# A decoder block with product-key experts: 32 instead of 64 tokens by fetched rows, and another order of four steps

## The chip, the cores and the metric

The kernel runs on one core of one Trainium2 chip. Times are device microseconds (us) of one execution. TensorE multiplies (PE in the profile, PEld its weight loads), VectorE is DVE, ScalarE is ACT, GpSimd is POOL and issues the indirect DMAs, SyncE is SP and issues the other DMAs.

## The reference

512 tokens of width 1024, float32 throughout:

```
h   = adaLN(RMSNorm(x), c);  p = h @ W_in            # q | k | v | conv B, C, u
attn = sliding window (128), 8 query heads on 2 key heads, RMSNorm on q and k, rotary, sinks
conv = B * conv3_causal(C * u)
x  += gate1 * ([RMSNorm(attn) | RMSNorm(conv)] @ W_out)
h2  = adaLN(RMSNorm(x), c)
x  += gate2 * PEER(h2)
```

PEER has 16384 experts of one neuron each, an expert being a row of `u` and a row of `v`. A token has 8 heads; a head picks 16 of 128 keys on each of two sides, and then the 16 best of the 256 sums. So each token has 128 experts: `out = sum_k g_k * gelu(u_k . h2) * v_k`.

## The kernel before, in words

The float32 products are made of float32r parts: a helper (`split`, lines 175 to 177) has ACT write the high part `hi` and DVE the low part `lo` of every weight tile, and `mm3` (lines 197 to 202) issues three matmuls (L200, L201, L202) for each of 8 tiles of 128.

The tokens are dealt with in two ways. The first 384 (`TD`, three chunks of 128) are "dense": for them whole tables are multiplied. Expert number is 128*j + i in the order of the kernel, and `first()` (line 606) takes one of 128 columns j: it loads 512 KB of `u`, splits it, and makes 24 matmuls into `pa`, whose width is the number of dense tokens that are served so, `TU` = 384 - `HT` = 320. ACT puts a gelu on it. The first `SPILL` = 66 columns go out to memory in pairs (`Ad`) and come back later (`sp`), the others stay in a ring of 4 pairs (`ge`). `second()` (line 966) takes one column of `v`: it is loaded and split, and multiplied by the gated activations `w` of all three chunks in 18 matmuls of 512 (L977 to L979) into six PSUM banks that stay open over all 128 columns. The gates stand in `Gd`, which 24 steps of `build()` (line 902, 16 tokens each) make from the routing with one-hot products on DVE (L912 to L927) and 32 small matmuls each into `gps`.

The last 64 dense tokens (`HT`) do not get their `u` products from `first()`. `last_dense()` (line 780) fetches, for each of 64 steps, 128 rows of `u` by an indirect DMA on POOL (tile `row` from `in_uR` by `eH`, 512 KB) and makes one dot product in each partition on DVE (L778, by `hN`): a step serves 64 tokens with two experts each. `eH` and `wN` are moved between the two halves of the partitions by one small DMA each. What is left is a gating factor that goes into the routing slots (L794 to L802).

The last 128 tokens are "gathered" (`gathered()`, line 854): their routing (`route`, two halves of four heads), then 128 fetches of `u` rows with a dot each (L778, by `h2N`), and 128 fetches of `v` rows with a multiply-add each (L893). This runs beside the rest in portions: `todo` counts units, a step of the main loop adds some and the generator gives back what its pieces are put down at (1.4 for one top-16 search of five DVE operations, 1.9 for the second search, 2.5 for a lookup, 1.3 for a dot or multiply-add).

The order of the main part: 2 columns of `first()`; six lookups of the dense routing (line 810) with `LOOK` = 4 columns each and, from the second lookup on, two dots of `last_dense()` each; the turned routing of the three chunks (lines 822 to 835, PSUM tile `ijg`, then `jI`, `jl` and the slots); 24 builds (lines 1004 to 1016), the first 16 with two columns and three dots, the last 8 with one column, two dots at most and, from build 20, 1.7 units of `gathered()`; 6 more columns with 2.3 units each; then 66 columns of `second()` without a `first()` (1.85 units each, `PACE`), 56 with one (4.4 units each), and 6 more. The attention (lines 374 to 432) comes long before that: `attend1` makes the scores of 8 heads (`sc`, L383, 64 partitions deep, head group g in the upper or lower half of the partitions), `attend2` turns them (L415), copies them (L417) and multiplies by `vN` (`po`, L423, 64 columns of weights per group).

The order in each engine's queue is not quite that of the program text: a planner in the framework writes the queues when the program is built, by its own estimates of durations, taking the earliest step of the text that is ready. The chip is given the queues as written. `after(ins, mark)` adds a wait for another instruction, and `fetch` (line 767) makes row fetches wait for the last matmul of a `second()`.

Of the kernel before, what the change touches and what calls it, by code (L numbers as in the profile page):

```python
# [11 lines left out]
I32 = mybir.dt.int32  # L12
# [12 lines left out]
TD = ND * P  # L25
HT = 64
TU = TD - HT
# [7 lines left out]
GS = 32768.0  # L35
RING = 4
LOOK = 4
SPILL = 66
EARLY = 1
# [5 lines left out]
WHEN = (-1, 0, 2, 3)  # L45
PACE = (1.85, 4.4)

# [42 lines left out]
def body(tc, p):  # L90
# [283 lines left out]
    def attend1(n):  # L374
        k0 = 0 if n else P
        s = a1.tile([P, 8, 256], F32, tag="s", name="s", bufs=2)
        for g in range(2):
            gp = slice(64 * g, 64 * g + 64)
            for b2 in range(2):
                ps = bank("sc")  # L380
                for i in range(2):
                    b = 2 * b2 + i
                    nc.tensor.matmul(ps[:, i * 256 + k0:(i + 1) * 256], qT[gp, b, n * P:(n + 1) * P],  # L383
                                     kT[gp, (n - 1) * P + k0:(n + 1) * P], start=True, stop=True)
                for i in range(2):
# [21 lines left out]
    def attend2(n, s):  # L407
        k0 = 0 if n else P
        po = bank("po")
        ptr, pT = {}, {}  # L410

        def turned(h):
            ptr = bank("pT")
            for kb in range(k0 // P, 2):
                nc.tensor.transpose(ptr[:, kb * P:(kb + 1) * P], s[:, h, kb * P:(kb + 1) * P], ident)  # L415
            pT[h] = a1.tile([P, 256], F32, tag="pT", name="pT", bufs=4)
            nc.scalar.activation(pT[h][:, k0:], ptr[:, k0:256], AF.Copy)  # L417

        def product(h):
            g, b = divmod(h, 4)  # L420
            gp = slice(64 * g, 64 * g + 64)
            for kb in range(k0 // P, 2):
                nc.tensor.matmul(po[gp, b * P:(b + 1) * P], vN[:, n - 1 + kb, gp],  # L423
                                 pT[h][:, kb * P:(kb + 1) * P], start=(kb == k0 // P), stop=(kb == 1))
# [157 lines left out]
    for r, (dst, cs) in enumerate(((hN, slice(TU - HT, TD)), (h2N, slice(TD, T)))):  # L582
        pg = [bank("pg0"), bank("pg1")]
        for k in range(DC):
            b = mod[:, 24 + k:25 + k]
            f = fs[k]
            if r == 0:
                nc.scalar.activation(f[:, TU - HT:TU], f[:, TU:TD], AF.Identity, bias=b)
# [187 lines left out]
    def dot(a, t, h):  # L776
        junk = rt.tile([P, D], BF16, name="junk", **R2)
        nc.vector.scalar_tensor_tensor(junk, t, 1.0, h, op0=OP.mult, op1=OP.mult, accum_out=a)  # L778

    def last_dense():  # L780


        rows = []
        for k in range(HT):
            while len(rows) < min(k + 3, HT):
                rows.append(fetch(p["uR"], eH[:, len(rows):len(rows) + 1]))
            dot(aH[:, k:k + 1], rows[k], hN)
            rows[k] = None
            yield
        nc.scalar.activation(aH, aH, AF.Gelu_apprx_tanh)  # L790
        nc.sync.dma_start(wN[HT:P, 0:HT], aH[0:HT, :])
        nc.vector.tensor_copy(wN[HT:P, HT:P], aH[HT:P, :])
        yield
        nc.vector.tensor_mul(wN[HT:P, :], wN[HT:P, :], gN[HT:P, :])  # L794
        m = rt.tile([P, 1], F32, tag="mH", name="mH", bufs=1)
        nc.vector.tensor_reduce(sH[HT:P], wN[HT:P, :], axis=X, op=OP.max, apply_absolute_value=True)
        nc.vector.tensor_scalar_max(sH[HT:P], sH[HT:P], 1e-30)
        nc.vector.reciprocal(m[HT:P], sH[HT:P])
        nc.vector.tensor_scalar_mul(wN[HT:P, :], wN[HT:P, :], m[HT:P])
        pt = bank("wH")  # L800
        nc.tensor.transpose(pt[:, 0:P], wN, ident)
        gate_parts(slice(TU, TD), pt[:, HT:P])  # L802

# [4 lines left out]
    gN = pp.tile([P, P], F32, name="gN")  # L808
    ahead = None
    for n, _ in enumerate(lookup(ND, Rd)):  # L810
        if n == 1:
            ei = rt.tile([P, P], I32, tag="rest", name="ei", bufs=2)
            numbers(ei, Rd, ND - 1)
            nc.sync.dma_start(eH[0:HT, :], ei[HT:P, 0:HT])
            nc.vector.tensor_copy(eH[HT:P, :], ei[HT:P, HT:P])
            nc.vector.tensor_copy(gN, Rd["g"][:, ND - 1].rearrange("p a b -> p (a b)"))
            ahead = last_dense()
        for k in range(LOOK):
            first()
            if ahead and k % 2:  # L820
                next(ahead)
    for c in range(ND):
# [7 lines left out]
        jl = rp.tile([P, P], I32, tag="jl", name="jl", bufs=2)  # L830
# [71 lines left out]
    def build(bt):  # L902

        if bt % 2 == 0:
# [3 lines left out]
            H = gb.tile([P, 32, 8, 4], F16, name="H", bufs=1)  # L908
            L, L1, L2 = [gb.tile([P, 32, 4, 4], F16, name=n, bufs=1) for n in ("L", "L1", "L2")]
            sl = [P, 32, 4, 4]  # L910
# [5 lines left out]
            nc.vector.tensor_mul(L1, L, x[:, 3, :, None].to_broadcast(sl))  # L916
            nc.vector.tensor_mul(L2, L, x[:, 4, :, None].to_broadcast(sl))
            low[0] = x, H, L1, L2
        x, H, L1, L2 = low[0]
# [84 lines left out]
    for bt in range(nb):  # L1004
# [105 lines left out]
```

## Time and profile before

| | |
|---|---|
| time, median of 3 runs | 1457.55 us (1456.76 to 1459.31) |
| the profiled execution, its own time | 1467.2 us |
| its span, first to last instruction | 1465.2 us |
| PE busy | 1379.4 us (94%) |
| DVE busy | 1270.6 us (87%) |
| ACT busy | 615.8 us (42%) |
| DMA moved | 432.72 MB, mean 295 GB/s |
| mean granted TensorE clock | 0.981 |

PE's busy time comes from modelled ends of pipelined matmuls, so it overstates how full PE is: how many matmuls ran in a stretch, against the stretch's length, says more. The profiled execution was 9.65 us longer than the median of the runs.

### The profile page before, as it was taken

The page shows a single profiled execution, that of the slowest core. Times are in us where ns is not written, and L with a number is a line of the kernel's source. Part 1 is how long each engine was busy: PE and PEld are TensorE (multiplying, and loading weights), DVE is VectorE, ACT ScalarE, POOL GpSimd, SP SyncE. Part 2 cuts the span into 40 slices and gives each one's busy share as a digit, 9 for nine tenths or more (in the row PEclk, how much of TensorE's full clock was granted, in tenths as well). Part 3 has the DMA queues.
Part 4 walks back from the last instruction along what each step waited for, and adds up shares of the span by engine and source line. Part 5 has one row for each costly group of instructions (what it writes and reads, how often), then busy time and mean ns, then how long its engine had stood idle before and what let it go on. Part 6 is the DMA issues. An engine that isn't in the chain of part 4 may idle for free.

```text
span 1465.2 us, 21360 instructions
## 1 busy us (share of the span) xinstructions
PE 1379.4 (94%) x7696; PEld 1196.9 (82%) x7696; DVE 1270.6 (87%) x2331; ACT 615.8 (42%) x1041; POOL 451.8 (31%) x324
## 2 busy tenths in 40 slices
PE   6999998999888999989999999999989998999998
PEld 4777776788888999878778888788879987888887
DVE  6778978799987999999898788997788988897885
ACT  4534546433733655545344343343334333333331
POOL 0000000000055044400312444555655645556610
PEclk9999999999999999999999999999999999999999
DMA  8645535232599799987998999999999999999963
GB/s 277 226 162 172 185 120 191 82 98 77 177 335 349 272 391 410 396 328 276 373 354 287 368 401 384 380 369 387 340 385 399 355 389 332 388 336 357 354 224 129
DMA packets 138570, 432.72 MB, mean 295 GB/s; under 512 B 13152, under 2 KB 39904, under 8 KB 136928
## 3 DMA queue, kind: packets, MB, share of 16 engines
q1 hardware_dynamic: 92384, 263.57, 49.8%
q0 software_dynamic: 46080, 167.79, 30.0%
q8 instruction: 60, 0.98, 0.3%
q14 instruction: 46, 0.38, 0.1%
HBM read 391.11 MB, written 40.17 MB: 294 GB/s over the span
## 4 chain that ended last, share of the span: by engine, by line
PE 43%; DVE 26%; DMA 13%; issue 11%; POOL 4%; ACT 2%; SPq 0%; DVEq 0%; POOLq 0%; ACTq 0%
DVE lo L177 6%; DMA row<-in_uR,eG 6%; PE o L978 5%; PE o L979 5%; PE o L977 5%; POOL row L770 4%; PE pa L202 4%; PE pa L200 4%; PE pa L201 4%; DVE junk L778 3%; DMA row<-in_vL,eG 3%; DMA row<-in_uR,eH 3%; PE pj L200 2%; PE pj L202 2%; PE pj L201 2%
## 5 line engine op out<-in xcount | busy, mean ns | idle before, releaser
L176 ACT ACTIVATE hi<-raw 128x1024 fp32r<-128x1024 f32 x298 | 311.6, 1053 | 311.6 <-PE pa L201 113.0
L177 DVE TENSOR_TENSOR lo<-raw,hi 128x1024 fp32r<-128x1024 f32 x298 | 362.1, 1217 | 34.8 <-ACT hi L176 29.3
L200 PE MATMUL pa<-h2H,hi 128*128 128x320 f32 x1024 | 321.8, 314 | 16.5 <-ACT sp L618 16.5
L202 PE MATMUL pa<-h2H,lo 128*128 128x320 f32 x1024 | 321.1, 314 | 12.1 <-DVE lo L177 11.8
L201 PE MATMUL pa<-h2L,hi 128*128 128x320 f32 x1024 | 319.6, 312 | 0.0
L978 PE MATMUL o<-lo,wwh 128*128 128x512 f32 x768 | 302.8, 394 | 15.9 <-DVE lo L177 15.8
L979 PE MATMUL o<-hi,wwl 128*128 128x512 f32 x768 | 301.9, 393 | 3.4 <-DVE wwl L177 3.2
L977 PE MATMUL o<-hi,wwh 128*128 128x512 f32 x768 | 301.8, 393 | 0.0
L770 POOL DMA_INDIRECT row<-in_uR,eG x128 | 173.4, 1354 | 286.2 <-PE o L979 122.6
L770 POOL DMA_INDIRECT row<-in_uR,eH x64 | 97.9, 1529 | 527.8 <-DVE eq L689 405.3
L770 POOL DMA_INDIRECT row<-in_vL,eG x128 | 180.3, 1409 | 132.5 <-DVE ga L893 79.7
L200 PEld LDWEIGHTS pa<-h2H,hi 128*128 128x128 f32 x1024 | 195.4, 191 | 20.2 <-ACT sp L618 17.8
L202 PEld LDWEIGHTS pa<-h2H,lo 128*128 128x128 f32 x1024 | 195.1, 191 | 15.3 <-DVE lo L177 15.3
L778 DVE SCALAR_TENSOR_TENSOR junk<-row,h2N 128x1024 bf16<-128x1024 f32 x128 | 153.5, 1220 | 54.9 <-DMA row<-in_uR,eG 48.2
L201 PEld LDWEIGHTS pa<-h2L,hi 128*128 128x128 f32 x1024 | 195.0, 190 | 2.2
L893 DVE SCALAR_TENSOR_TENSOR ga<-row,av,ga 128x1024 f32<-128x1024 f32 x127 | 163.0, 1283 | 32.1 <-DMA row<-in_vL,eG 30.9
L978 PEld LDWEIGHTS o<-lo,wwh 128*128 128x128 f32 x768 | 145.4, 189 | 49.2 <-DVE lo L177 20.5
L979 PEld LDWEIGHTS o<-hi,wwl 128*128 128x128 f32 x768 | 145.2, 189 | 36.3 <-DVE wwl L177 6.0
L977 PEld LDWEIGHTS o<-hi,wwh 128*128 128x128 f32 x768 | 145.4, 189 | 29.0 <-issue 0.2
L959 ACT ACTIVATE w<-G 128x64 f32<-128x64 f32 x128 | 25.8, 249 | 322.6 <-DVE wwl L177 318.5
L778 DVE SCALAR_TENSOR_TENSOR junk<-row,hN 128x1024 bf16<-128x1024 f32 x64 | 77.6, 1215 | 17.1 <-DMA row<-in_uR,eH 16.6
L176 ACT ACTIVATE wwh<-w 128x768 fp32r<-128x768 f32 x64 | 53.8, 841 | 65.0 <-PE o L978 61.4
(265 smaller groups left out, 1867.9 us busy)
## 6 DMA issues: line engine op xcount, KB each, us to landing
raw<-in_uL SPq DMA_DIRECT2D x128, 512.0 KB
raw<-in_vL SPq DMA_DIRECT2D x128, 512.0 KB
Gd<-st SPq DMA_DIRECT2D x12, 2048.0 KB
G<-Gd SPq DMA_DIRECT2D x16, 1536.0 KB
ada<-in_ada SPq DMA_DIRECT2D x32, 512.0 KB
Ad<-sp SPq DMA_DIRECT2D x33, 320.0 KB
sp<-Ad SPq DMA_DIRECT2D x33, 320.0 KB
raw<-in_w_in SPq DMA_DIRECT2D x18, 512.0 KB
```

The source lines that it names most:

```text
L176: nc.scalar.activation(h, f, AF.Copy)
L177: nc.vector.tensor_sub(l, f, h.bitcast(F32))
L200: nc.tensor.matmul(ps, wh(k), rh(k), start=(k == k0), stop=False)
L201: nc.tensor.matmul(ps, wh(k), rl(k), start=False, stop=False)
L202: mark[0] = nc.tensor.matmul(ps, wl(k), rh(k), start=False, stop=(k == k1))
L770: d = nc.gpsimd.indirect_dma_start(out=t, out_offset=None, in_=tab, in_offset=bass.IndirectOffsetOnAxis(ap=e, axis=0))
L778: nc.vector.scalar_tensor_tensor(junk, t, 1.0, h, op0=OP.mult, op1=OP.mult, accum_out=a)
L893: nc.vector.scalar_tensor_tensor(ga, t, av[:, k:k + 1], ga, op0=OP.mult, op1=OP.add)
L959: nc.scalar.activation(wv[:, i, nu:], g[:, i, nu:], AF.Copy)
L977: nc.tensor.matmul(o, wh[:, cs], vh[:, hs], start=(j == 0), stop=False)
L978: nc.tensor.matmul(o, wh[:, cs], vl[:, hs], start=False, stop=False)
L979: last = nc.tensor.matmul(o, wl[:, cs], vh[:, hs], start=False, stop=(j == NJ - 1))
```

## The change

`HT` goes from 64 to 32, so `TU` from 320 to 352: `first()` is 352 wide, and 32 fetches with a dot each are left, a fetch now serving 32 tokens with four experts each. `hN` holds the last 32 dense tokens four times; `eH` and `wN` are moved by three small DMAs each instead of one. `RING` 4 to 3, `LOOK` 4 to 3 with three columns put behind the turned routing, `SPILL` 66 to 68, `PACE` (1.85, 4.4) to (1.75, 4.2).

The dots of `last_dense()` start at the fourth lookup instead of the second (two per lookup, six in all), with four rows in flight instead of three, and each waits by `after` for a mark: in the lookups the last matmul three columns back, later the last slot of the third chunk's turned routing. `jI` and `jl` get three buffers instead of two. When `last_dense()` is used up (at build 8 or 9), `gathered()` starts with 2.5 units per build, where it started at build 20 with 1.7. In `build`, `L2` is written over `L`.

In the attention, the scores of the two head groups alternate (two PSUM banks are taken at once), and so do the products with `vN`, which come in groups of both heads.

```diff
-HT = 64
+HT = 32
-RING = 4
-LOOK = 4
-SPILL = 66
+RING = 3
+LOOK = 3
+SPILL = 68
-PACE = (1.85, 4.4)
+PACE = (1.75, 4.2)
...
-        for g in range(2):
-            gp = slice(64 * g, 64 * g + 64)
-            for b2 in range(2):
-                ps = bank("sc")
-                for i in range(2):
-                    b = 2 * b2 + i
+        for b2 in range(2):
+            pss = [bank("sc") for g in range(2)]
+            for i in range(2):
+                b = 2 * b2 + i
+                for g, ps in enumerate(pss):
+                    gp = slice(64 * g, 64 * g + 64)
                     nc.tensor.matmul(ps[:, i * 256 + k0:(i + 1) * 256], qT[gp, b, n * P:(n + 1) * P],
                                      kT[gp, (n - 1) * P + k0:(n + 1) * P], start=True, stop=True)
...
-        for h in range(8):
-            turned(h)
-            if h > 2:
-                product(h - 3)
-        for h in range(5, 8):
-            product(h)
+        for b in range(4):
+            turned(b)
+            turned(b + 4)
+            if b > 0:
+                products(b - 1)
+        products(3)
...
-            while len(rows) < min(k + 3, HT):
+            while len(rows) < min(k + 4, HT):
                 rows.append(fetch(p["uR"], eH[:, len(rows):len(rows) + 1]))
-            dot(aH[:, k:k + 1], rows[k], hN)
+            after(dot(aH[:, k:k + 1], rows[k], hN), held[0])
...
         for k in range(LOOK):
+            ends.append(mark[0])
             first()
-            if ahead and k % 2:
+            if n > 2 and k < 2:
+                held[0] = ends[-3]
                 next(ahead)
...
-        jI = rp.tile([P, P], I32, tag="jI", name="jI", bufs=2)
+        jI = rp.tile([P, P], I32, tag="jI", name="jI", bufs=ND)
...
-        nc.vector.tensor_sub(jhT[:, cs], jI, jl)
+        held[0] = nc.vector.tensor_sub(jhT[:, cs], jI, jl)
...
+    for k in range(3):
+        first()
     rp_s.close()
...
         for k in range(2 if bt < nb - LAST else 1):
-            next(ahead, None)
+            left = next(ahead, 0) is None
             first()
-        next(ahead, None)
-        if bt >= TU // 16:
-            todo += 1.7
+        if not left:
+            todo += 2.5
             while todo > 0:
                 todo -= next(gth)
```

## Rows read from the trace of the kernel before

**Rows 1.** Windows, all engines by stage (columns: stretch, length, busy and count, PEclk, DMA share, GB/s)

```profile
360.00:402.00 42.00, 36.47 (x238) 35.95 (x237) 41.46 (x126) 28.09 (x31) 1.85 (x2) 0.96 0.53 160
402.00:482.00 80.00, 67.20 (x429) 66.50 (x428) 64.48 (x103) 25.81 (x45) 40.35 (x28) 0.91 0.95 339
482.00:571.00 89.00, 88.83 (x818) 87.19 (x818) 88.36 (x111) 51.84 (x88) 28.86 (x19) 1.00 0.91 353
571.00:699.00 128.00, 116.44 (x994) 110.40 (x992) 126.68 (x267) 67.38 (x117) 26.83 (x17) 0.97 0.90 342
699.00:972.00 273.00, 269.00 (x1172) 220.04 (x1171) 236.83 (x406) 105.33 (x167) 105.53 (x81) 0.99 0.97 364
972.00:1430.00 458.00, 435.70 (x2353) 389.14 (x2352) 393.78 (x404) 163.82 (x255) 248.15 (x176) 0.99 0.94 354
```

**Rows 2.** Windows, PE alone on tile pa, the matmuls of first()

```profile
424.00:460.00 36.00, 36.00 (x248) 1.00 0.99 374
402.00:482.00 80.00, 66.46 (x420) 0.91 0.95 339
482.00:571.00 89.00, 71.16 (x462) 1.00 0.91 353
571.00:699.00 128.00, 90.83 (x576) 0.97 0.90 342
972.00:1430.00 458.00, 208.28 (x1344) 0.99 0.94 354
```

**Rows 3.** Windows, PE alone on tile o, the matmuls of second()

```profile
780.00:880.00 100.00, 100.00 (x443) 1.00 0.98 367
972.00:1430.00 458.00, 245.45 (x1009) 0.99 0.94 354
```

**Rows 4.** Windows, PE alone on tile gps, the matmuls of build()

```profile
482.00:571.00 89.00, 22.26 (x356) 1.00 0.91 353
571.00:699.00 128.00, 29.53 (x416) 0.97 0.90 342
```

**Rows 5.** Waits from 400 to 482 us (us in total, times, longest)

```profile
DVE junk L778 <- DMA row<-in_uR,eH: 15.0, 7, 6.0
ACT jI L829 <- DVE slots L833: 11.1, 1, 11.1
PE pa L200 <- ACT sp L618: 8.0, 1, 8.0
PE pa L202 <- DVE lo L177: 4.3, 1, 4.3
```

**Rows 6.** The dots of last_dense() up to 482 us (ns min/median/max, first and last start)

```profile
L778 DVE SCALAR_TENSOR_TENSOR junk<-row,hN x25: 1212/1218/1228, 408.3 to 475.9; 128x1024 bf16<-128x1024 f32 x25
```

**Rows 7.** Waits from 970 to 1430 us

```profile
DVE ga L893 <- DMA row<-in_vL,eG: 30.9, 11, 7.3
PE o L978 <- DVE lo L177: 15.2, 9, 5.1
```

**Rows 8.** Windows, all engines, within the two stages of second()

```profile
840.00:960.00 120.00, 119.20 (x524) 97.81 (x523) 104.78 (x142) 44.59 (x73) 55.99 (x41) 1.00 1.01 390
```

**Rows 9.** Chain of waits (start us, us, what): attention, then DVE on end

```profile
128.89 2.90 PE sc L383 x16
184.70 1.91 PE po L423 x16
1053.23 2.29 DVE junk L778 x4
1092.42 1.15 DVE lo L177
```

**Rows 10.** Groups of instructions (count, busy us, mean ns, idle before)

```profile
L383 PE MATMUL sc<-kT,qT 64*128 64x256 f32 x48 | 9.2, 391 | 0.0
L423 PE MATMUL po<-pT,vN 128*64 128x128 f32 x112 | 16.9, 282 | 0.9 <-DVE s L387 0.5 <-ACT pT L417 0.3
L629 DVE MAX8 V<-rest 128x8 f32<-128x128 f32 x64 | 18.0, 281 | 0.2
```

More of the change, by code (lines that the diff above doesn't have):

```diff
@@ L376, in attend1 @@
         s = a1.tile([P, 8, 256], F32, tag="s", name="s", bufs=2)
-        for g in range(2):
-            gp = slice(64 * g, 64 * g + 64)
-            for b2 in range(2):
-                ps = bank("sc")
-                for i in range(2):
-                    b = 2 * b2 + i
+        for b2 in range(2):
[4 more added lines that the diff above has]
+                    gp = slice(64 * g, 64 * g + 64)
                     nc.tensor.matmul(ps[:, i * 256 + k0:(i + 1) * 256], qT[gp, b, n * P:(n + 1) * P],
                                      kT[gp, (n - 1) * P + k0:(n + 1) * P], start=True, stop=True)
+            for g, ps in enumerate(pss):
                 for i in range(2):
@@ L417, in turned, with products @@
             nc.scalar.activation(pT[h][:, k0:], ptr[:, k0:256], AF.Copy)
-        def product(h):
-            g, b = divmod(h, 4)
-            gp = slice(64 * g, 64 * g + 64)
+        def products(b):
             for kb in range(k0 // P, 2):
-                nc.tensor.matmul(po[gp, b * P:(b + 1) * P], vN[:, n - 1 + kb, gp],
-                                 pT[h][:, kb * P:(kb + 1) * P], start=(kb == k0 // P), stop=(kb == 1))
-        for h in range(8):
-            turned(h)
-            if h > 2:
-                product(h - 3)
-        for h in range(5, 8):
-            product(h)
+                for g in range(2):
+                    gp = slice(64 * g, 64 * g + 64)
+                    nc.tensor.matmul(po[gp, b * P:(b + 1) * P], vN[:, n - 1 + kb, gp],
+                                     pT[b + 4 * g][:, kb * P:(kb + 1) * P], start=(kb == k0 // P), stop=(kb == 1))
+        for b in range(4):
[4 more added lines that the diff above has]
+        products(3)
         nc.scalar.activation(attnT[:, :, n * P:(n + 1) * P], po.rearrange("p (a b) -> p a b", a=4), AF.Copy)
@@ L581, in body @@
             mm3(o, w, lambda k: fH[:, k, :], lambda k: fL[:, k, :], [k])
-    for r, (dst, cs) in enumerate(((hN, slice(TU - HT, TD)), (h2N, slice(TD, T)))):
+    for r, (dst, cs) in enumerate(((hN, slice(TD - P, TD)), (h2N, slice(TD, T)))):
         pg = [bank("pg0"), bank("pg1")]
@@ L777, in dot @@
         junk = rt.tile([P, D], BF16, name="junk", **R2)
-        nc.vector.scalar_tensor_tensor(junk, t, 1.0, h, op0=OP.mult, op1=OP.mult, accum_out=a)
+        return nc.vector.scalar_tensor_tensor(junk, t, 1.0, h, op0=OP.mult, op1=OP.mult, accum_out=a)
+    held = [None]
     def last_dense():
@@ L790, in last_dense @@
         nc.scalar.activation(aH, aH, AF.Gelu_apprx_tanh)
-        nc.sync.dma_start(wN[HT:P, 0:HT], aH[0:HT, :])
-        nc.vector.tensor_copy(wN[HT:P, HT:P], aH[HT:P, :])
+        for q in range(0, P - HT, HT):
+            nc.sync.dma_start(wN[P - HT:P, q:q + HT], aH[q:q + HT, :])
+        nc.vector.tensor_copy(wN[P - HT:P, P - HT:P], aH[P - HT:P, :])
         yield
-        nc.vector.tensor_mul(wN[HT:P, :], wN[HT:P, :], gN[HT:P, :])
+        nc.vector.tensor_mul(wN[P - HT:P, :], wN[P - HT:P, :], gN[P - HT:P, :])
         m = rt.tile([P, 1], F32, tag="mH", name="mH", bufs=1)
[L796 to L799, printed above, removed]
+        nc.vector.tensor_reduce(sH[P - HT:P], wN[P - HT:P, :], axis=X, op=OP.max, apply_absolute_value=True)
+        nc.vector.tensor_scalar_max(sH[P - HT:P], sH[P - HT:P], 1e-30)
+        nc.vector.reciprocal(m[P - HT:P], sH[P - HT:P])
+        nc.vector.tensor_scalar_mul(wN[P - HT:P, :], wN[P - HT:P, :], m[P - HT:P])
         pt = bank("wH")
         nc.tensor.transpose(pt[:, 0:P], wN, ident)
-        gate_parts(slice(TU, TD), pt[:, HT:P])
+        gate_parts(slice(TU, TD), pt[:, P - HT:P])
     def gate_parts(cs, src):
@@ L809, in body @@
     ahead = None
+    ends = []
     for n, _ in enumerate(lookup(ND, Rd)):
@@ L813, in body @@
             numbers(ei, Rd, ND - 1)
-            nc.sync.dma_start(eH[0:HT, :], ei[HT:P, 0:HT])
-            nc.vector.tensor_copy(eH[HT:P, :], ei[HT:P, HT:P])
+            for q in range(0, P - HT, HT):
+                nc.sync.dma_start(eH[q:q + HT, :], ei[P - HT:P, q:q + HT])
+            nc.vector.tensor_copy(eH[P - HT:P, :], ei[P - HT:P, P - HT:P])
             nc.vector.tensor_copy(gN, Rd["g"][:, ND - 1].rearrange("p a b -> p (a b)"))
@@ L908, in build @@
             H = gb.tile([P, 32, 8, 4], F16, name="H", bufs=1)
-            L, L1, L2 = [gb.tile([P, 32, 4, 4], F16, name=n, bufs=1) for n in ("L", "L1", "L2")]
+            L, L1 = [gb.tile([P, 32, 4, 4], F16, name=n, bufs=1) for n in ("L", "L1")]
             sl = [P, 32, 4, 4]
@@ L916, in build @@
             nc.vector.tensor_mul(L1, L, x[:, 3, :, None].to_broadcast(sl))
-            nc.vector.tensor_mul(L2, L, x[:, 4, :, None].to_broadcast(sl))
-            low[0] = x, H, L1, L2
+            nc.vector.tensor_mul(L, L, x[:, 4, :, None].to_broadcast(sl))
+            low[0] = x, H, L1, L
         x, H, L1, L2 = low[0]
```

5 lines of the change are left out of this document (3 added, 2 removed).

## The prediction

> **What bounds the kernel now.** I read the page first (PE 94%, DVE 87% busy), then cut the span into its stages with the windows view and counted matmuls, because PE's busy time is modelled. Where PE runs without a break, a `pa` matmul of 320 columns comes every 36.00/247 = 0.1457 us [rows 2] and an `o` matmul of 512 every 100/442 = 0.2262 us [rows 3]. In 482 to 571 us PE never waits, so its 356 `gps` matmuls take (89 - 462 x 0.1457)/356 = 0.061 us each [rows 2, 4]. Work against length by these pitches:
>
> 402 to 482 us (lookups, turned routing): 420 x 0.1457 + about 1 for nine transposes = 62 of 80 us; 18 idle or at the lower clock (PEclk 0.91) [rows 1, 2].
> 482 to 571 (first half of the builds): no idle time, but DVE too is full: 88.4 of 89 us, and the DMA share is 0.91 [rows 1].
> 571 to 699 (rest of the builds, six columns): 576 x 0.1457 + 416 x 0.061 = 109 of 128; 19 idle, DVE 126.7 of 128. DVE is the bound [rows 1, 2, 4].
> 699 to 972 (second() alone): 1172 matmuls, 265 of 273; PE is the bound; 8 idle [rows 1].
> 972 to 1430 (both): 1344 x 0.1457 + 1009 x 0.2262 = 424 of 458; 34 idle [rows 2, 3].
>
> The waits say what ends the idle time. In the lookups a dot sits first in DVE's queue while its row is on its way (15.0 us in 7 waits), and a `lo` behind it makes PE wait 4.3 us. Then ACT holds `jI` for 11.1 us until DVE, busy with dots, frees its buffer; the gelus behind it on ACT are late and PE waits 8.0 us [rows 5]. In the last stage DVE waits 30.9 us for rows of `v`, and PE waits for a `lo` behind them [rows 7]. So PE is the bound by work, and most of its idle time comes from the fetched rows that the change halves or moves.
>
> **The change part by part.** *Wider u.* From the two pitches a column costs (0.2262 - 0.1457)/192 = 0.000419 us, so 32 cost 0.0134: a `pa` matmul comes every 0.1591 us, a column of first() takes 3.82 us for 3.50, and 3072 matmuls cost 41.2 us more, 22.8 of it in the 71 columns between 360 and 699 us and 18.0 in the 56 after 972. No idle time hides this where PE is the bound.
>
> *Fewer dots.* 32 dots, 32 fetches and 32 x 0.524 MB go. Dots start 1.145 us apart (2.29 for two) and a `lo` takes as much [rows 9]: 36.6 us of DVE.
>
> *Attention.* 48 score records of 256 columns and 112 product records [rows 10]. A block of 16 score records takes 2.90 us though they change the head group only once [rows 9]; around that change the records start closer together, so alternation can bring a block to about 1.9: at most 1 us in each of four blocks. For the products no row shows two groups side by side; 16 in one run take 1.91 us [rows 9]. Bounds for them: the same overlap, half of 112 x 0.119 = 6.7 us, or nothing, or 1 us lost by taking two banks at once and all four `pT` buffers. I take -2 for the scores and -1 for the products, nearest to the row that shows no overlap: -3 (from -9 to +1). The Trainium skill's TensorEngine Tiling (Array Packing), section Key Properties, says that different tiles of the array run independently; by it both would overlap and the sum would be -9.
>
> *Lookups.* The dots begin two lookups later and behind a mark, so no dot should be first in DVE's queue with its row still under way; with three `jI` buffers ACT no longer stops. Of the 18 us I let 15 go (12.3 of waits [rows 5] and the low clock behind them). The new wait: behind the waiting dot stand the next lookup step and the next `lo`, for which PE waits; the mark is three columns back, two columns (7.6 us) before PE needs that `lo`, so it costs nothing; if the mark came a column late in each of six dots it would cost up to 6 x 3.8 = 23. So from 360 us: 22 columns x 3.82 + 1 + 3.5 idle (as in 360 to 402: 42 - 11 x 3.5 [rows 1]) + 3 = 91.5; the builds start at 451.5, for 482 before, but with 23 columns done instead of 28.
>
> *Builds.* DVE's sum from there: 215 us before [rows 1]; of the 64 dots 25 were done before 482 [rows 6], 39 stood behind, now 26: -14.9; five more `lo`: +5.7; gathered() now gets 15 x 2.5 + 9 x 2.3 = 58.2 units for 20.6. A top-16 search of five operations of 0.281 us [rows 10] is put down at 1.4, so a unit is 1 us by durations and some 0.8 by starts (a dot lasts 1.218 but starts 1.145 apart [rows 6, 9]): +30 (up to +38). Sum 236. PE's sum: 49 x 3.82 + 768 x 0.061 = 234. Both are nearly the same, and they do not peak together: the last eight builds now ask about 7.4 us of DVE (2.0 routing, 1.15 `lo`, the rest one-hots) and 5.8 of PE. 8 x 1.6 = 13, less a build that stands ready: I add 11 to 236 and get 247. So second() starts at 451.5 + 247 = 698.5, for 699: no gain (from -13 with PE alone as the bound to +12 with units of 1 us and more mismatch).
>
> *second() alone.* Two columns more, 67 for 65 here: 1206 x 0.2262 = 273; idle 8 to 4, as the second half of the routing is done earlier: 277 for 273, +4. Its DMA: gathered rows run from its start, 119/1.3 = 91 instead of 81 [rows 1], two more columns, wider spills: 99.4 + 5.5 + 1.8 + 1.1 = 108 MB. In 840 to 960 the same mix ran at 390 GB/s with PE full (119.2 of 120) [rows 8]: 277 us. It just fits.
>
> *Both.* PE: 1344 x 0.1591 + 1008 x 0.2262 = 442. Idle time was 34, 0.6 us in each step of a fetching stretch. A step asks 4.2 units for 4.4 (3.2 rows for 3.4) and lasts 7.9 us for 7.6, so bytes per us fall by about 7%, and rows are used up some 5 steps earlier (204/4.2 = 49 for 238/4.4 = 54). Bounds for the idle time: 7 to all 34; I take 17, half: 459 for 458, +1. RING and the shorter lead (4 columns for 6) leave 4 x 7.9 us between gelu and use: nothing. Behind 1430, two steps less: -8.
>
> The small DMAs on SP (three for one, twice), wider copies on ACT and DVE (`w`, `h2H`, slots) and `L2` over `L` lie beside PE work on engines with room, at nothing; without that cover about 3 us.
>
> Sum: -3 + 0 + 4 + 1 - 8 = -6 to -7 against the profiled 1467.2 us: 1460.5. The runs' median is 9.65 us below that execution, so I scale: 1460.5 x 1457.55/1467.2 = 1451.
>
> **The rivals.** *The rows' waits stay (slower).* In the last stage DVE may wait for a row's latency rather than for bandwidth: the queue's order is written beforehand, and each `ga` ahead of its row holds the `lo` behind it, however much the DMA engines have to spare. Then 34 us of idle time stay and 18 are added: 17 worse than my term, 1467 + 10 = 1477, scaled 1468. For it: 11 waits of up to 7.3 us [rows 7] with a DMA share of 0.94, not 1. Against: in 840 to 960 PE hardly waits, at 1.01 [rows 8]. It decides from about 27 us of idle time upward.
>
> *second() alone becomes DMA-bound (no change).* 108 MB at 364/0.97 = 375 GB/s [rows 1] are 288 us, +11: scaled 1461, half of that 1456 to 1459. The Trainium skill's DMA: Bandwidth & Descriptors, section Where 436 GB/s comes from, puts the limit from memory at about 358 GB/s: 302 us and 1475. The trace disagrees, with 390 GB/s over 120 us [rows 8]; I give that rule 2 in 100, inside the slower case.
>
> *Nearly all idle time goes (faster still).* Builds at PE's sum plus little (-10), 7 us of idle time at the end (-10): 1441 profiled, scaled 1431 to 1437. For it: each row wait is tied to the rows that go. Against: DVE's and PE's sums in the builds are equal.
>
> *The order doesn't change as said:* if the planner still puts dots ahead of the turned routing, the 15 us stay: 1466; part of the slower case.
>
> **How the numbers follow.** Forecast (1441 to 1456) 0.45, nearly all gone 0.14, no change 0.18, slower 0.23. 0.2% is 2.9 us, about what a measurement of this kernel can tell from no change. Faster: 0.14 + 0.45 with a little moved either way = 0.59; within 0.2%: 0.18; slower 0.23. The range, 1436 to 1468, leaves out half of the best case and what lies beyond the slower rival; the likeliest's own is 1441 to 1456.
>
> **What would show it.** `pa` at 0.159 us in a stretch without idle time; no `jI` wait of 11 us and builds starting near 452 us; second() starting near 698, PE idle about 22 us between; 277 us of second() alone; idle time in the last stage near 17 us and a DMA share below 0.94. Wrong it is if `pa` costs more than columns (then all terms of 18 and 23 grow), if the dots hold DVE on their marks, or if the last stage keeps its 34 us.

## The result, and the profile after

The changed kernel took 1452.57 us (median of six runs, 1451.00 to 1453.08), the kernel before 1458.36 (six, 1456.62 to 1459.41). The ratio is 0.9948, with an interval of 0.9925 to 0.9972: 7.6 us faster, 4 to 11 by the interval. The forecast was 1451, so direction and size are right. Its terms were not all right; errors of opposite sign cancel, and the experiments below are mostly about these.

The profiled execution of after took 1453.08 us (span 1451.3), 0.5 us over its median. That of before was 8.8 us over its median, so differences between the two traces are too large by that much. The excess is mainly in the last stage: from the first to the last `pa` matmul it took 454 us there, but 446 and 448 us in two runs whose code, and the order of whose DVE queue, are the same in that stage (experiments 1 and 4). The first `pa` moves from one trace to the next as well (experiment 1), so a row of this table is good to a few us.

Stages are cut at the first `pa` matmul of the main part, the first `gps`, the first `o`, the first `pa` behind that, and the last `pa`:

| stage, us in the trace | before | forecast | after |
|---|---|---|---|
| up to the first `pa` | 353.4 | 350 | 349.3 |
| lookups, turned routing | 128.7 | 98 | 102.3 |
| builds and the columns behind them | 216.8 | 247 | 253.0 |
| second() alone | 277.1 | 281 | 278.2 |
| both | 454.0 | 455 | 441.3 |
| behind the last `pa` | 35.2 | 27 | 27.2 |

The windows view of after, all engines, answers to [rows 1] with the stages cut at its own marks (columns as there: stretch, length, busy and count of PE, PEld, DVE, ACT, POOL, then PEclk, DMA share, GB/s):

```profile
349.00:452.00 103.00, 94.85 (x575) 93.50 (x575) 99.53 (x324) 51.84 (x72) 16.55 (x13) 0.97 0.64 213
452.00:705.00 253.00, 237.79 (x1946) 233.61 (x1946) 236.76 (x421) 130.71 (x223) 56.31 (x36) 0.97 0.90 328
705.00:983.00 278.00, 277.68 (x1226) 229.58 (x1225) 226.50 (x294) 104.27 (x169) 117.37 (x83) 1.00 0.98 371
983.00:1424.00 441.00, 440.32 (x2333) 400.50 (x2332) 369.48 (x359) 162.84 (x249) 214.88 (x156) 1.00 0.91 343
```

Look at the last row first: PE is busy in 440.3 of 441 us at a granted clock of 1.00. The same stage of before, between the same marks:

```profile
976.00:1430.00 454.00, 431.70 (x2335) 385.82 (x2334) 389.99 (x399) 163.31 (x253) 246.21 (x174) 0.98 0.94 354
```

There PE was busy in 431.7 of 454 us at a granted clock of 0.98. At the pitches that the prediction used (56 x 24 matmuls of 0.1591 us, 55 x 18 of 0.2262) the work of this stage is 437.7 us, so 3.6 us of idle time are left, where 17 were forecast.

The pitch itself can be checked in a stretch of the lookups. The windows view of after on PE's `pa` matmuls answers to the first line of [rows 2]; PE is busy all the time and 188 matmuls start in 30 us, one each 30/187 = 0.160 us (forecast 0.159):

```profile
405.00:435.00 30.00, 30.00 (x188) 1.00 0.86 305
```

The waits of after in the last stage, which answer to [rows 7] (engine, line, releaser: us in total, times, longest), and under them two lines of the same view of before, from 976 to 1430 us, that are not among those rows:

```profile
DVE ga L905 <- DMA row<-in_vL,eG: 24.5, 10, 4.4
DVE junk L781 <- DMA row<-in_uR,eG: 16.6, 6, 5.4
PE pa L202 <- DVE lo L177: 0.4, 1, 0.4
PE o L990 <- DVE lo L177: 0.2, 1, 0.2
```

```profile
DVE junk L778 <- DMA row<-in_uR,eG: 14.1, 6, 4.2
PE pa L202 <- DVE lo L177: 6.9, 5, 3.7
```

DVE still waits 41 us for fetched rows (before 30.9 + 14.1 = 45). PE's waits for `lo` fell from 15.2 + 6.9 = 22 us to 0.6. So DVE still waits for rows, and PE no longer feels it. That is not what the prediction said would happen.

In the builds new waits have come. Two lines of the waits view of after from 452 to 705 us:

```profile
ACT x L919 <- DVE A L935: 54.2, 10, 12.6
PE pa L200 <- ACT sp L621: 14.3, 4, 6.6
```

And ACT's instructions around the two longest of PE's gelu waits, from the timeline of after (start, us, instruction, in brackets what it waited for):

```profile
613.49 0.73 ACT L919 ACTIVATE x<-slots 128x640 f16<-128x640 f16 x1 [12.56 <-DVE A L935]
615.08 0.44 ACT L621 ACTIVATE sp<-pa 128x352 f32<-128x352 f32 x1
...
669.09 0.31 ACT L702 ACTIVATE Rg<-Rg 128x128 f32<-128x128 f32 x1 [3.15 <-DVE Rg L701]
672.19 1.06 ACT L668 ACTIVATE ex<-I 128x1024 f16<-128x1024 uint32 x1 [2.79 <-DVE eq L689]
673.26 1.28 ACT L621 ACT_TABLE_LOAD   x1
674.56 0.47 ACT L621 ACTIVATE sp<-pa 128x352 f32<-128x352 f32 x1
```

In both cases the gelu (`sp`) comes after other instructions in ACT's queue. In the first a copy for a later build stands ahead of the gelu and waits 12.56 us for DVE, which has `gathered()` to do as well: three of its dots, 3.5 us, lie in that wait by DVE's timeline. In the second the exponential of the gathered routing (L702) and a copy of its lookup (L668) wait 3.15 and 2.79 us for DVE, and a load of ACT's function table, 1.28 us, follows.

### The profile page after: what moved, and what is told of

It reads as the page before. It is cut to its first block, busy times and chain, and to the rows that moved or that the text cites. A ratio compares the mean times of both kernels' runs of the same rounds, so it can differ in the third digit from the quotient of the medians.

```text
span 1451.3 us, 21225 instructions
## 1 busy us (share of the span) xinstructions
PE 1394.5 (96%) x7696; PEld 1224.8 (84%) x7696; DVE 1240.8 (85%) x2267; ACT 616.3 (42%) x1041; POOL 405.3 (28%) x292
## 4 chain that ended last, share of the span: by engine, by line
PE 22%; issue 14%; POOL 8%; DMA 7%; DVE 5%; ACT 0%; POOLq 0%; DVEq 0%; ACTq 0%
POOL row L773 8%; DMA row<-in_uR,eG 5%; PE pa L200 4%; PE pa L202 4%; PE pa L201 4%; PE o L990 3%; PE o L991 3%; PE o L989 3%; DMA row<-in_vL,eG 2%; DVE lo L177 2%; DVE junk L781 1%; DVE wwl L177 0%; DVE ga L905 0%; DMA raw<-in_vL 0%; DVE x L1008 0%
## 5 line engine op out<-in xcount | busy, mean ns | idle before, releaser
L200 PE MATMUL pa<-h2H,hi 128*128 128x352 f32 x1024 | 336.1, 328 | 21.1 <-ACT sp L621 21.1
L202 PE MATMUL pa<-h2H,lo 128*128 128x352 f32 x1024 | 332.8, 325 | 0.4 <-DVE lo L177 0.4
L201 PE MATMUL pa<-h2L,hi 128*128 128x352 f32 x1024 | 332.0, 324 | 0.0
L990 PE MATMUL o<-lo,wwh 128*128 128x512 f32 x768 | 299.1, 389 | 0.2 <-DVE lo L177 0.2
L991 PE MATMUL o<-hi,wwl 128*128 128x512 f32 x768 | 298.9, 389 | 0.3 <-DVE wwl L177 0.3
L773 POOL DMA_INDIRECT row<-in_uR,eG x128 | 188.9, 1476 | 326.1 <-PE o L991 165.7
L773 POOL DMA_INDIRECT row<-in_vL,eG x128 | 171.7, 1341 | 145.6 <-PE o L991 91.3
L773 POOL DMA_INDIRECT row<-in_uR,eH x32 | 44.5, 1392 | 489.3 <-ACT sp L621 394.8
L991 PEld LDWEIGHTS o<-hi,wwl 128*128 128x128 f32 x768 | 144.1, 188 | 30.9 <-DVE wwl L177 0.7
L971 ACT ACTIVATE w<-G 128x32 f32<-128x32 f32 x128 | 22.3, 222 | 196.3 <-DVE wwl L177 191.6
L177 DVE TENSOR_TENSOR wwl<-w,wwh 128x768 fp32r<-128x768 f32 x64 | 60.8, 951 | 10.5 <-ACT wwh L176 10.5
```

Of the source, the lines that this page charges most:

```text
L177: nc.vector.tensor_sub(l, f, h.bitcast(F32))
L200: nc.tensor.matmul(ps, wh(k), rh(k), start=(k == k0), stop=False)
L201: nc.tensor.matmul(ps, wh(k), rl(k), start=False, stop=False)
L202: mark[0] = nc.tensor.matmul(ps, wl(k), rh(k), start=False, stop=(k == k1))
L773: d = nc.gpsimd.indirect_dma_start(out=t, out_offset=None, in_=tab, in_offset=bass.IndirectOffsetOnAxis(ap=e, axis=0))
L971: nc.scalar.activation(wv[:, i, nu:], g[:, i, nu:], AF.Copy)
```

## The experiments

Ratios are to the kernel before, measured on the same chip, with a 95% interval.

**1. The attention alone,** in the kernel before.

```diff
-        for g in range(2):
-            gp = slice(64 * g, 64 * g + 64)
-            for b2 in range(2):
-                ps = bank("sc")
...
+        for b2 in range(2):
+            pss = [bank("sc") for g in range(2)]
...
-        for h in range(8):
-            turned(h)
-            if h > 2:
-                product(h - 3)
+        for b in range(4):
+            turned(b)
+            turned(b + 4)
+            if b > 0:
+                products(b - 1)
...
```

> The kernel before with the attention's new order alone (scores and products of the two head groups alternate). Theory: worth 3 to 5 us, the first matmul of first() comes near 349 us instead of 353, and all behind it moves with it: 1453 to 1455 beside 1458. Rival, the attention is hidden by the conv projections beside it or the gain is given back at a later wait: 1457 to 1459.

0.9951 (0.9931 to 0.9971): 7 us (4 to 10 by the interval), where the forecast had 3. The marks bear the 7 out: the first `pa` starts at 351.0 to 358.2 us in the six traces with the old order (before and experiments 3, 4, 5, 9, 10) and at 344.4 to 349.3 in the eight with the new one, with means 6.9 us apart. The timeline of PE in after shows how (start, us to the last record's end, instruction, records in a run), with the groups of the same two lines, which answer to [rows 10]:

```profile
107.89 2.00 PE L383 MATMUL sc<-kT,qT 64*128 64x256 f32 x16
177.45 0.66 PE L425 MATMUL po<-pT,vN 128*64 128x128 f32 x8
```

```profile
L383 PE MATMUL sc<-kT,qT 64*128 64x256 f32 x48 | 6.0, 389 | 0.0
L425 PE MATMUL po<-pT,vN 128*64 128x128 f32 x112 | 11.0, 296 | 1.0 <-DVE s L388 1.0
```

A record is as long as before (389 for 391 ns, 296 for 282), but the busy time, which counts overlapped records once, fell from 9.2 to 6.0 and from 16.9 to 11.0 us: 3.2 + 5.9 = 9. Those ends are modelled, but the starts say the same: in after the records of these two runs start in pairs, one of each group, 0.006 to 0.007 us apart, and from the second pair on a pair follows a pair in 0.216 us (scores) or 0.109 (products), the time from one record to the next in a run of one group in before. A block of 16 score records takes 2.00 us for 2.90 [rows 9], and eight products fit in 0.66, where 16 took 1.91 [rows 9]. The two head groups run side by side in the scores and in the products.

**2. The changed kernel at width 320,** with 64 rows.

```diff
-HT = 32
+HT = 64
```

> The changed kernel with HT = 64 again (u 320 wide, 64 fetched rows), all other edits kept. Theory, 32 rows more fetched cost in waits what the narrower u saves in matmuls: builds start near 443 us, but dots fill them until build 19, DVE has some 14 us more to do there than PE, and the last stage gets back 15 to 30 us of idle time: 1450 to 1458. Rival, the width itself was a loss and other edits gave the gain: about 41 us of PE work go and little idle time comes, 1420 to 1440.

0.9967 (0.9947 to 0.9986), which this run alone can't tell from after. The stages move, though: the builds take 272 us (445.7 to 717.6) for 253, as 56 of the 64 dots lie behind the first build (24 of 32 in after) and DVE does them beside the one-hots. PE's wait for `lo` in the builds, of which after has none:

```profile
PE pa L202 <- DVE lo L177: 19.4, 5, 6.7
```

The width costs PE 23 us more up to there and 18 in the last stage, but takes that DVE work away. The last stage took 428 us, 8 of them idle, where I had expected 15 to 30.

**3. The width alone,** in the kernel before (with what it needs: `RING` 3, `SPILL` 68, `L2` over `L`, the three small moves).

```diff
-HT = 64
+HT = 32
...
-RING = 4
+RING = 3
...
-SPILL = 66
+SPILL = 68
...
```

> The kernel before with HT = 32 and what the memory then asks for (RING 3, SPILL 68, L2 over L); attention, lookups, jI, pace and the start of gathered() as before. Theory: 41 us more of matmuls against idle time that goes: in the builds DVE has 36 us less to do, so the 19 idle us before second() go but the 23 of matmuls come; in the last stage the units per us fall from 0.58 to 0.555 as in the kernel before with the new pace, which left about 10 us of idle time there, so 15 to 20 go and 18 come: 1453 to 1465 beside 1459. Rival, the width is the gain of the change: 1440 to 1450. Second rival, idle time comes from other causes and stays: 1480 to 1500.

1.0092 (1.0058 to 1.0125): 13 us slower, outside what I expected. The windows of its builds and of its last stage:

```profile
497.00:714.00 217.00, 212.05 (x1801) 208.11 (x1800) 191.01 (x410) 121.50 (x208) 4.42 (x4) 0.99 0.76 278
992.00:1445.00 453.00, 445.24 (x2336) 403.54 (x2335) 391.01 (x397) 163.16 (x250) 240.68 (x174) 0.99 0.94 355
```

In the builds DVE now has 26 us of room and nothing to put in it. In the lookups the dots still sit in DVE's queue ahead of what PE needs (ACT's wait for DVE's slots is 18.9 us here, for 11.1 before [rows 5]). In the last stage PE has 437.7 us of work, and 15 us are idle, for 26 to 28 in experiments 1 and 4: the width takes near half of the idle time and pays for it in matmuls.

**4. The `jI` buffers alone,** in the kernel before.

```diff
-        jI = rp.tile([P, P], I32, tag="jI", name="jI", bufs=2)
+        jI = rp.tile([P, P], I32, tag="jI", name="jI", bufs=ND)
```

(and `jl` the same.)

> The kernel before with three buffers for jI and jl instead of two, nothing else. Theory, the dots ahead in DVE's queue are the cause of the stop in the turned routing: ACT no longer waits 11 us for jI, but the slots still come behind the dots on DVE, the first build stays near 480 us, and the time falls by 0 to 2 us (1456 to 1458). Rival, the buffer itself was the cause: PE's wait of 8 us and the low clock behind it go, 1447 to 1450.

1.0013 (0.9989 to 1.0037): nothing. The waits of this kernel from 400 to 482 us, beside [rows 5]:

```profile
DVE junk L778 <- DMA row<-in_uR,eH: 12.1, 9, 3.5
ACT x L907 <- DVE slots L833: 10.8, 1, 10.8
PE pa L200 <- ACT sp L618: 9.1, 1, 9.1
```

ACT's wait for `slots` has moved from `jI` to the next instruction that needs DVE, and PE's wait for the gelu behind it is still 9 us. The buffer only named the wait: without it ACT stops just as long at the next thing that DVE has to deliver, behind the dots in DVE's queue.

**5. The new pace alone,** in the kernel before.

```diff
-PACE = (1.85, 4.4)
+PACE = (1.75, 4.2)
```

> The kernel before with PACE (1.75, 4.2) alone. Theory, the idle time of the last stage comes with rows per us: 4.2 units instead of 4.4 lower the load by 4%, and the rest of the rows is left for the end: 1452 to 1458, idle time in the last stage 20 to 30 us. Rival, the pace alone makes the last stage run without idle time: 1430 to 1442.

0.9891 (0.9858 to 0.9925): 16 us (11 to 21 by the interval) from two constants which the prediction had counted only as part of the bytes asked for per us. My expectation fell; the median, 1441.73, is at the upper end of the rival's. The last stage of this kernel, in an execution 6.6 us below that median:

```profile
968.00:1398.00 430.00, 425.15 (x2335) 382.44 (x2335) 383.59 (x399) 161.37 (x252) 259.57 (x178) 1.00 0.98 373
```

PE's own work here is 419.7 us (56 x 24 x 0.1457 + 55 x 18 x 0.2262), so the idle time is 10 us in this execution, for 34 in the profile of before and 26 to 28 in experiments 1 and 4. The DMA engines run at a share of 0.98 and 373 GB/s, more than before (0.94, 354 [rows 1]): the faster kernel is the one with the busier DMA.

**6. The changed kernel at the old pace.**

```diff
-PACE = (1.75, 4.2)
+PACE = (1.85, 4.4)
```

> The changed kernel with PACE (1.85, 4.4) again. Theory, idle time follows the units per us: 4.4 in 7.93 us is 0.555, what the kernel before with the new pace had (4.2 in 7.56), so 5 to 12 us of idle time come back in the last stage: 1455 to 1465. Rival, idle time follows the units of a step whatever its length: 25 us come back, 1472 to 1480. Second rival, with u 352 wide the pace no longer matters: 1450 to 1454.

0.9988 (0.9970 to 1.0006), so with 32 rows the pace is worth about 6 us (0.9948 against 0.9988, with intervals that just meet), not 16. Its last stage took 448.0 us with 10 idle, after's 441.3 with 4. With experiment 3 this splits the change along one path: width +13; attention and order together -15 (1.0092 to 0.9988), of which experiment 1 gives -7 to the attention; pace -6. The sum is -8. The -8 that are left for the order were not split further: the late dots were not run alone with 32 rows.

**7. gathered() late,** as in the kernel before, in the changed one.

```diff
-        if not left:
-            todo += 2.5
+        if not left and bt >= 20:
+            todo += 1.7
```

> The changed kernel with gathered() started at build 20 with 1.7 units again (2.3 in the columns behind, as in both), all else kept. Theory, the early start is what fills DVE and ACT in the builds: the two waits of 6 us for a gelu go, second() starts at 688 to 695 us instead of 704, and the 31 units moved to the end just fit (56 steps of 4.2): 1440 to 1448. Rival, DVE's sum there is no bound and the moved units cost as much at the end: 1451 to 1458.

0.9952 (0.9932 to 0.9972): no difference from after, and I had expected a gain. But the edit moved less than its text says. By the `scg` tile on DVE the searches of `gathered()` start at 421.1 us, for 423.0 in after and 646.3 in before: the planner, which takes the earliest step that is ready, had put them ahead all the same. Mainly dots moved: 10 instead of 17 stand ahead of `second()`, 81 instead of 98 ahead of the last stage. The long gelu wait of the builds, which I had put down to the early start, is still there, 6.3 us for 6.6 (this kernel from 451 to 699.5 us):

```profile
ACT x L919 <- DVE A L935: 50.8, 10, 12.2
PE pa L200 <- ACT sp L621: 11.3, 5, 6.3
```

The builds took 248.6 us for 253.0 and the last stage 443.0 for 441.3: of the 4 us that the builds give, 2 are gone again at the end, and what is left is less than this comparison can tell. What a `gathered()` that starts late on the chip would do was not measured.

**8. Late dots with 64 rows:** the kernel before with attention and pace of after, and the dots of `last_dense()` behind the marks (with three `jI` buffers).

```diff
-            dot(aH[:, k:k + 1], rows[k], hN)
+            after(dot(aH[:, k:k + 1], rows[k], hN), held[0])
...
-            if ahead and k % 2:
+            if n > 2 and k < 2:
+                held[0] = ends[-3]
                 next(ahead)
```

> The kernel before (64 rows, u 320 wide, LOOK 4) with three of the change's edits: the attention's order, PACE (1.75, 4.2), and the late, marked dots with three jI buffers. Attention and pace were worth 7 and 18 us alone. Theory, with 64 rows the late dots only move work: builds start some 15 us earlier, but 58 dots instead of 39 stand behind that point and cost DVE 22 us more, which it has no room for: 1430 to 1442, no better than attention and pace together. Rival, the stops in the lookups were lost time and stay away: 1415 to 1425.

0.9976 (0.9957 to 0.9996), against 0.9844 without the late dots (experiment 11): 19 us lost, more than either expectation (the median is 1455.78). The builds start 14 us earlier (460.1 for 473.7), but the last `gps` is at 686.4 for 664.5. From 460 to 710 us ACT waits for tables of `u`, with the gelus behind it, and PE waits for the gelus (in experiment 11 these two are 12.1 and 3.5 us); the last two lines are the waits around the end of the builds:

```profile
ACT hi L176 <- DMA raw<-in_uL: 45.3, 14, 7.4
PE pa L200 <- ACT sp L620: 21.1, 17, 3.0
...
PE o L984 <- ACT wwh L176: 12.7, 1, 12.7
...
DVE w L967 <- DMA G<-Gd: 5.9, 1, 5.9
```

Behind the last build comes a store of its gates to `Gd` and a load of the first `G`, with nothing left to cover them. So the 14 us that the lookups gain are lost in the builds, and more. Not all of it need be the dots: 57 of them and their fetches lie behind the first build for 39, but the planner also put all of `gathered()`'s searches ahead of `second()` (50 of 80 records in experiment 11).

**9. Half of each dot.** In the kernel before (pace 4.4) `gathered()` makes its dots and multiply-adds on half of each row, so half of the gathered sums is left out; the fetches are whole.

```diff
-            dot(av[:, k:k + 1], row(k, 2 * P if routed else P // 2), h2N)
+            dot(av[:, k:k + 1], row(k, 2 * P if routed else P // 2)[:, 0:D // 2], h2N[:, 0:D // 2])
```

(and the multiply-adds the same.)

> The kernel before where gathered()'s dots and multiply-adds on VectorE use the first half of each row only (0.6 us instead of 1.2); the fetches stay whole. Left out: half of the gathered tokens' sums. The pace stays 4.4. Theory, the last stage's idle time is DVE waiting for rows that 16 DMA engines cannot bring faster: DVE has time to spare but still stands ahead of each row, so 15 to 30 us of idle time stay there (454 us by the profile of before, 446 to 448 in two others; here 440 or more). Rival, DVE's own sum is the bound: it falls by 2 us in a step and the idle time goes, 425 to 432.

0.9855 (0.9833 to 0.9876). This is the run that says most on the last stage: my expectation fell and the rival's held (425 to 432). Its last stage, and the waits in it:

```profile
970.00:1397.00 427.00, 423.54 (x2332) 382.11 (x2331) 298.37 (x399) 164.97 (x252) 201.20 (x174) 1.00 0.97 374
```

```profile
DVE ga L894 <- DMA row<-in_vL,eG: 68.9, 20, 7.7
DVE junk L778 <- DMA row<-in_uR,eG: 36.2, 9, 8.1
...
PE o L979 <- DVE lo L177: 2.0, 2, 1.1
PE pa L202 <- DVE lo L177: 1.5, 2, 1.1
```

DVE waits 105 us for rows, more than twice as long as before, with the same bytes, and PE waits 3.5 us. The rows need not come later for that: DVE is at them sooner. If its waits for rows were all that counts, PE would wait longer here than in any other run. DVE's own work fell from 390 to 298 us, and after a wait it catches up before PE needs the next `lo`. Worked out from the timelines, the median time from the end of a `lo` to the first matmul that reads it is 3.7 us here, for 1.8 in before. One thing changed beside it: DVE's queue is in another order than before's, as the planner goes by estimated durations.

**10. Half of each row as well:** the same, with 2 KB fetched from each row of 4 (half of the sums left out, as in 9; `fetch` gets a width for it).

```diff
-                rows.append(fetch(vR if q else p["uR"], ei[:, i:i + 1]))
+                rows.append(fetch(vR if q else p["uR"], ei[:, i:i + 1], D // 2))
```

> As the half dots, and gathered()'s fetches bring half rows too (2 KB instead of 4, as many fetches; other rows than the reference's). Theory, bytes are what binds the last stage: 0.9 MB less in a step, and the idle time goes, last stage 424 to 432 us. Rival, it is a fetch's latency and its place in DVE's queue, not bytes: idle time stays, 440 or more.

0.9820 (0.9787 to 0.9852). The last stage:

```profile
975.00:1397.00 422.00, 422.00 (x2332) 382.07 (x2331) 299.32 (x395) 166.69 (x252) 212.80 (x174) 1.00 0.79 268
```

28% fewer bytes per us (268 for 374 GB/s) go with idle time of 3 us for 8; the times of the two kernels can't be told apart (medians 1434.51 and 1436.37, four runs each). DVE still waits 102 us for rows, and the median lead of a `lo` is 6.7 us. This is what fewer bytes are worth once DVE has room; half rows with whole dots, which would show what they are worth to a full DVE, were not run.

**11. Attention and pace,** in the kernel before, nothing else.

> The kernel before with the attention's order and PACE (1.75, 4.2), nothing else of the change: what the single runs point to. They touch different stages (before 190 us and after 970 us), so they should add: 7 + 17, 1433 to 1438. If one of them needs the other's place: 1439 to 1445.

0.9844 (0.9821 to 0.9868), median 1434.30: the best version, 23 us under before and 15 to 18 under the changed kernel (by the ratios, by the medians). The two parts add as they should (7 + 16). Its last stage and the waits there:

```profile
965.00:1395.00 430.00, 425.17 (x2333) 382.25 (x2332) 381.43 (x399) 160.34 (x251) 267.04 (x178) 1.00 0.98 374
```

```profile
DVE ga L895 <- DMA row<-in_vL,eG: 29.8, 11, 5.6
...
PE pa L202 <- DVE lo L177: 2.3, 2, 1.9
PE o L980 <- DVE lo L177: 2.2, 4, 0.9
```

DVE's waits for rows of `v` are those of before (29.8 for 30.9 us); PE's waits are 4.5 us.

**12. The same with the pace of the last stage alone.**

```diff
-PACE = (1.85, 4.4)
+PACE = (1.85, 4.2)
```

on top of the attention.

> As the one before with PACE (1.85, 4.2): only the last stage is slowed, and second() alone keeps its 1.85. If rows per us of the last stage alone matter: 1431 to 1438, as good or a little better since fewer units are left at the end (57 steps of 56 instead of 58). If the pace of second() alone was part of the gain: 1440 to 1446.

0.9884 (0.9862 to 0.9906): 6 us behind experiment 11 by the ratios, 8 by the medians (1442.26), as the second branch had it. The last stage has 20 us of idle time for 10 with both constants, but this execution was 6.6 us over its median, so the difference is too large by some of that:

```profile
971.00:1411.00 440.00, 428.26 (x2333) 383.57 (x2332) 384.28 (x396) 161.11 (x253) 248.95 (x174) 1.00 0.97 362
```

So a part of the gain seems to hang on the 1.85 of the stage before, where PE hardly waits with either. Its path into the last stage (which rows are in flight, where the order of the queues shifts) was not tried on its own and stays open.

## Why the prediction was right, and where it was not

**Where the last stage's time went.** The prediction put the 34 us of idle time down to rows that come late, let half go because fewer bytes are asked for per us, and so came to 17. The size is wrong (3.6) and so is the lever. Experiment 9 has DVE waiting longer for rows than any other run, with PE nearly full; experiment 10 gives the bytes 5 us once DVE has room. What experiment 9 changed is the room that DVE has in a step. A step of 24 + 18 matmuls is 24 x 0.1457 + 18 x 0.2262 = 7.6 us, and DVE is busy in 390 of 454 us, 7.0 in each of 56 steps. With 0.6 us of room, a row that is 5 us late is made good only over some eight steps. The width makes a step 0.3 us longer, which lifts the room by half; in after DVE is busy in 6.6 us (369.5/56) of a step of 7.9, twice the room, also because 159 row operations (dots and multiply-adds) stand in this stage for 178, the rest being done earlier. The median lead of a `lo` there is 4.1 us for 1.8. That the 16 us of pace are only 6 on top of the width fits this: both remove the same idle time.

How the pace does it alone is not shown. It takes 0.2 units (0.15 of a dot, 0.2 us) from a step, but what it leaves over comes later: experiment 5 has 177 row operations in this stage for 178, spread to its end, where before was through 19 us earlier. DVE is busy in 383.6 us for 390.0, 0.1 us less in a step, and the median lead is 2.1 us for 1.8. The order of DVE's queue in this stage differs from before's in every run that changed the pace, the width or the dots, and no run changes the order alone; how much is room and how much is order stays open.

The windows view of before in pieces of 10 us shows a place where a late row gets through to PE:

```profile
1210.00:1220.00 10.00, 9.04 (x50) 7.65 (x48) 4.41 (x5) 5.69 (x9) 6.87 (x5) 1.00 0.89 299
1220.00:1230.00 10.00, 5.76 (x18) 4.58 (x19) 9.93 (x10) 0.00 (x0) 5.41 (x4) 0.66 0.83 292
...
1280.00:1290.00 10.00, 7.84 (x33) 6.67 (x34) 9.93 (x10) 5.68 (x9) 4.54 (x3) 0.83 0.91 320
```

First DVE stands still (busy in 4.41 of 10 us; it waits 5.6 us for a row of `v`), then it is full (9.93) and PE waits 5.1 us for the `lo` behind, and the granted clock is at the 1.2 GHz level for two thirds of the stretch (0.66). Part of that stretch is the wait itself, in which a low clock costs nothing:

```profile
1221.10:1224.20 3.10, 0.00 (x0) 0.00 (x0) 3.06 (x4) 0.00 (x0) 2.32 (x2) 0.50 0.84 284
1224.20:1227.90 3.70, 3.66 (x9) 2.88 (x10) 3.70 (x4) 0.00 (x0) 2.67 (x3) 0.50 0.82 290
```

PE worked for 3.7 us at half the clock, which costs 1.9 us. The same follows a wait of 2.6 us (0.83, the row of 1280 to 1290 above; 3.4 us of work, 1.7 lost) and one of 3.7 (2.8 us of work, 1.4 lost), 5 us in all beside the waits. With PE's waits for `lo`, 15.2 us in `o` [rows 7] and 6.9 in `pa`, that makes 27 of the 34; in after the clock stays at 1.00. The step that failed is the sentence that most of PE's idle time "comes from the fetched rows": a row starts the delay, but by experiment 9 more room on DVE takes PE's waits from 22 to 3.5 us with the rows as they were.

**Attention.** The forecast was -3, measured -7 alone. The direction is right; the terms were mis-sized, above all that for the products (-1, where the busy time of that line fell by 5.9), because no row showed two groups side by side in them and I took the value nearest to that. The Trainium skill's TensorEngine Tiling (Array Packing), section Key Properties, says that different tiles run independently; by it the sum was -9, and the busy time of the two lines fell by 9. The trace agrees with the page on both lines; the whole kernel gained 7.

**Lookups.** The builds start at 451.6 us, as forecast to 0.1, but that is luck: the forecast did not have the attention's 4 us (in this pair of traces) in it, and the stage itself took 102.3 us for 98. Not foreseen was that the planner would put half of `gathered()`'s searches here (40 of 80 records, from 423.0 us); DVE is busy in 99.5 of 103 us. No dot waits long for its row (2.4 us in two waits, for 15.0 in seven [rows 5]), and the 11 us wait of ACT is gone; three gelu waits of up to 3.1 us, 6.8 in all, are new. The buffers of `jI`, which the prediction credited with a part, do nothing by themselves (experiment 4).

**Builds.** 253 us for 247. DVE's 236.8 us are the sum that was forecast (236), but of other parts: half of the searches in it were done in the lookups, and 17 of `gathered()`'s dots and eight more `lo` than before (51 for 43; five were forecast) came in (and a unit by starts, put at 0.8, is 1.145/1.3 = 0.88 for a dot). The mismatch between the engines was put at 11 and is 16; PE's gelu waits there are 14.3 us, 6.6 the longest. That the stages up to second() bring "no gain" was right: it starts at 704.6, 6 us later than before.

**second() alone.** 278.2 us, 1.1 more than before for two more columns (forecast +4). PE is busy in 277.7 of 278, so the rival that this stage becomes bound by DMA did not come; it moved 371 GB/s for 278 us.

**Behind the last `pa`.** 27.2 for 35.2: -8, as forecast.

**The sum.** Against the trace the errors are -1 (attention), +4 (lookups), +6 (builds), -3 (second() alone), -14 (both), together -8 to a forecast of 1460.5: 1453. Some 6 to 8 of the 14 were never in the code: the profiled execution of before was long in just that stage, and scaling to the median took those off again. So the time is right by luck, because errors cancel: lookups and builds 10 worse than forecast, the last stage and the rest about as much better in the code itself.

**The rivals.** "The rows' waits stay" had the mechanism half right (they stay on DVE: 41 us, and 102 with half the bytes in experiment 10) and the price wrong, as PE does not feel them. "Nearly all idle time goes" is what happened to the last stage, while the builds did not give their part.

## What to carry to other kernels

A wait that the trace names is where a delay enters; whether it reaches the bound engine is a matter of how much room the engine in between has per step, so set its sum against the step before you blame the transfer. Two edits that feed from the same idle time don't add: measure each alone and on top of the other, since here the costly one (the width) was paid for by time that two constants took away for nothing. A cheap constant that sets how fast side work is mixed in deserves its own run before a structural change. And where a planner writes the queues, look in the trace whether an edit moved what its text moves (experiment 7) and what else it moved (experiments 5, 8 and 9).

## What the runs showed of the hardware

- Matmuls in two head groups overlapped when they alternated: eight product records of 128 columns in 0.66 us, where 16 took 1.91 in one run of a group; 48 score records busy for 6.0 us instead of 9.2, the two records of a pair starting 0.006 to 0.007 us apart.
- After waits of PE of 2.6 to 5.1 us the granted clock was 0.66 to 0.83 over 10 us; in the last stage of before that cost 5 us beside waits of 22.
- One core moved 371 to 374 GB/s for 278 to 430 us, with PE nearly full. The Trainium skill's DMA: Bandwidth & Descriptors, section Where 436 GB/s comes from, names about 358 GB/s as what binds for transfers between HBM, the chip's memory, and the core, half of the 716 GB/s that two cores share; the runs, with one core at work, are some 4% above it.
